# The decay of the first two heads of a linear attention is queued behind the projection of the keys instead of that of the values

## The chip, the cores and the metric

The kernel runs on one core of a Trainium2 chip. The metric is the time of one execution on the device in microseconds (us). The core has TensorE (PE; its weight loads are shown apart as PEld), VectorE (DVE), ScalarE (ACT), GpSimd (POOL) and SyncE (SP), which issues most transfers. Each engine works through its own list of instructions in order, and waits for the others through semaphores.

## The reference, cut to what matters

One decoder layer on 256 tokens of width 2048. Two kinds of attention read one projection of the normalised input: four heads of gated linear attention (GLA) and eight heads of a sparse attention (NSA). Their outputs go through one output projection, and a feed-forward block follows. Everything is float32.

```python
n = rms_norm(x, attn_norm_g)
proj = n @ w_in
(g_qkv, g_lr, g_out, nq, kc, vc, ks, vs, kw, vw, ng) = jnp.split(proj, offsets, axis=-1)
g_qkv = jax.nn.silu(causal_short_conv(g_qkv, gla_conv_w))
gq, gk, gv = jnp.split(g_qkv, [GLA_QK, 2 * GLA_QK], axis=-1)
gla_out = gla_mixer(gq, gk, gv, g_lr, g_out, gla_gate_w2, gla_gate_b, gla_norm_g)
nsa_out = nsa_mixer(nq, kc, vc, ks, vs, kw, vw, ng, ...)
h = x + jnp.concatenate([gla_out, nsa_out], axis=-1) @ w_out
m = rms_norm(h, ffn_norm_g)
return h + (jax.nn.silu(m @ w_gate) * (m @ w_up)) @ w_down
```

In the GLA, a gate gives every key channel a logarithmic decay for each token, `log_a`. A score between a query at t and a key at s is a product of their channels, weighted by the exponential of the decay summed from s to t:

```python
b = jnp.cumsum(gi, axis=2)
decay = jnp.exp(jnp.where(causal, b[:, :, :, None, :] - b[:, :, None, :, :], -jnp.inf))
scores = jnp.einsum('bhtd,bhsd,bhtsd->bhts', qi, ki, decay)
o_intra = jnp.einsum('bhts,bhse->bhte', scores, vi)
```

So the decay needs the gate, and its product with queries and keys needs those two; it needs no values. The values enter with `o_intra`.

## The kernel before

**Matrix products.** Each float32 matrix product is made of three passes: operands are split into a high part (hi) and a rest (lo), and hi x hi, hi x lo and lo x hi are added in PSUM. A projection (`proj`, L291) covers 512 columns of the weights: for 16 blocks of 128 rows and 2 blocks of 128 tokens it issues three matmuls, 96 in all, each 512 columns wide. Weights come in raw tiles of 4 row blocks (tag "raw", 3 buffers, loaded by SP at L128), and `split` (L131) makes for every 2 row blocks a hi tile on ACT (L137) and a lo tile on DVE (L138), with 4 buffers each. A raw buffer is free when its lo parts are made, and a hi or lo buffer when TensorE is done with it.

**Order of the projections.** The low-rank gate with half of the output gate; the other half of the output gate; queries; keys; first half of the values; second half of the values (these are columns 0, 512, 1024 and 1536); then for the NSA the keys of the compression, of the selection and of the window, and two halves of the queries. Then comes the output projection in two halves (`w_out_half`): the first reads the GLA's outputs, the second those of the NSA. After that comes the feed-forward block.

**Side work.** All else is written as generators that hand back control at each `yield`. `drive` (L98) runs the projections; every matmul yields 2 units, and whenever the credit reaches the pace, `side` (L83) advances one generator by one step: the first in the list `urgent`, or, when that is empty, the first in the list `later`. At pace 1.5 a projection offers 128 steps, at 2.5 76.8. Where both lists are empty, steps pass unused. A third list, `background`, is advanced by a count of units of its own: `sum_rows` loads weights of the feed-forward block on SP (L1041), adds rows of them on DVE (L1046) and stores the sums by POOL (L1050).

**Planner.** The generators only set the order in which instructions are written down. A planner of the framework then places them on their engines: an instruction that is ready may go ahead of earlier written ones that are not. Tiles of one tag share a number of buffers. The tag "g2" (a 4 KB-and-smaller working tile of SBUF) has 13.

**The GLA around the change.** `gla_gate` (L428) is in `later` from the first projection on; it leaves the gate's logarithms in `dec["f"]`, and `dec["r"]` zeroed. After queries, keys and each half of the values, `conv` (L481) is put in `urgent`: it turns the projection on TensorE, runs the short convolution (L490 on ACT, L492 on DVE) and ends with Silu on ACT, in `to_qk` (L500; L502 and L503) and, for values, `to_v` (L507; L510 and L511), which turns them back (L521). `gla_decay(hp)` (L526) serves the heads 2 hp and 2 hp + 1. For 7 block lengths it takes two Exp on ACT (L542, L544), updates running sums r and f on DVE (L548, L550) and multiplies by keys and queries on DVE (L552 or L554, L555), with two steps of nothing after each half: 28 steps, and one more for the part across chunks (L560 to L564). It fills 8 tiles of the tag "g2". It issues no matmul and no DMA. `gla_scores` (L567) multiplies these tiles on TensorE (L581) and picks blocks on DVE (L576); `gla_out` (L599) multiplies by the values (L604 to L608); `gla_turn` (L625) turns the result for the output projection. `gla_mix` (L644) runs all this for four heads: the decay of heads 0 and 1, four empty steps, then scores and outputs, with the decay of heads 2 and 3 interleaved with the scores of head 1.

**Where it is queued.** `gla_mix` enters `later` after the second half of the values, before the NSA projections begin. There, `compress` (L736) is put behind it, and `nsa_mix` (L917) after that. At the end of the first half of the output projection both lists are drained, so all of it must be written by then.

Of the kernel before, what the change touches and what calls it, by code (L numbers as in the profile page):

```python
# [33 lines left out]
C_LR, C_GO, C_NQ, C_KC, C_KS, C_KW, C_NG = 2048, 2064, 3088, 4112, 4624, 5136, 5648  # L34
# [3 lines left out]
def kernel(  # L38
# [30 lines left out]
    def bank():  # L69
        n_tiles[0] += 1  # L70
        return pp.tile([P, 512], F32, tag="bank", name=f"bank_{n_tiles[0]}")

    def behind(op):

        return tc.issue_after(op.ins) if op is not None else nullcontext()
# [5 lines left out]
    urgent, later, background = [], [], []  # L81

    def side():  # L83

        for queue in (urgent, later):
            while queue:
                try:
                    next(queue[0])
                    return
                except StopIteration:  # L90
                    queue.pop(0)
# [6 lines left out]
    def drive(mains, pace):  # L98

        credit = 0.0  # L100
        for m in mains:
            for units in m:
                count[0] += units
                if background and 0 < rate[0] <= count[0]:
                    count[0] = 0
                    if next(background[0], None) is None:
                        background.pop(0)
                credit += units
                while credit >= pace:
                    side()  # L110
                    credit -= pace
# [19 lines left out]
    def split(r, nk, w, k0=0, fine=False):  # L131

        res = []
        for k in range(k0, nk, 2):
            h, o = weight("hi", 2, w, 4), weight("lo", 2, w, 4)
            for i, n in ((0, 1), (1, 1)) if fine else ((0, 2),):
                act(h[:, i:i + n], r[:, k + i:k + i + n], AF.Copy)  # L137
                last["d"] = TT(o[:, i:i + n], r[:, k + i:k + i + n], f32(h[:, i:i + n]), ALU.subtract)  # L138
            res += [(h[:, 0], o[:, 0]), (h[:, 1], o[:, 1])]
        return res  # L140

    def fetch(mat, k0, nk, c0, w):
        return load(mat[k0 * P:(k0 + nk) * P, c0:c0 + w].rearrange("(k p) w -> p k w", p=P), nk, w)
# [65 lines left out]
    def transpose(o, i, n=P):  # L209
        return nc.tensor.transpose(o, i, ident[:n, :n])  # L210
# [80 lines left out]
    def proj(c0, evac, parts=((0, 512),), start=None):  # L291

        w = parts[-1][0] + parts[-1][1]
        banks = [[bank()[:, :pw] for _ in range(NT)] for _, pw in parts]
        ws = start(0) if start else None
        for q in range(NQ):
            if not start:
                ws = split(fetch(wi, 4 * q, 4, c0, w), 4, w)
            for i, u in enumerate(chunk(banks, n_h[q], n_l[q], ws, q == 0, q == 3, parts)):
                yield u  # L300
                if start and q == 0 and i == 5:
                    with behind(last["mm"]):
                        next(first_rest)
                if start and i == (12 if q == 0 else 6) and q < 3:
                    with behind(last["mm"] if q == 0 else None):
                        nxt = start(q + 1)
            if start and q < 3:
                ws = nxt
        evac(banks)
# [64 lines left out]
    def ev_go(b):  # L374
        def f(banks):
            if b == 0:
                lr = small([NT, 16])
                for t in range(NT):
                    TS(lr[:, t, :], banks[0][t][:, 0:16], rx[:, t:t + 1], None, ALU.mult)
            for t in range(NT):  # L380
                at = 0
                for bk in banks:
                    src = bk[t][:, 16:] if b == 0 and at == 0 else bk[t]
                    n = src.shape[1]
                    act(gout[b][:, t, at:at + n], src, AF.Silu, scale=rx[:, t:t + 1])
                    at += n
            if b == 0:
                later.append(gla_gate(lr))
        return f
# [72 lines left out]
    kk, qq = (g4([2, 2, 2, P]) for _ in range(2))  # L462
# [12 lines left out]
    def scaled(banks):  # L475
        u = g4([NT, 512])
        for t in range(NT):
            act(u[:, t, :], banks[0][t], AF.Copy, scale=rx[:, t:t + 1])
        return u
# [15 lines left out]
    def ev_conv(ct, dst):  # L495
        def f(banks):
            urgent.append(conv(scaled(banks), ct, dst))
        return f

    def to_qk(near, far):  # L500
        def f(pair, y):
            act(near[:, pair, 0 if near is kk else 1], y[:, :, 0:P], AF.Silu)  # L502
            act(far[:, pair, 0 if far is qq else 1], y[:, :, S - 1:P - 1:-1], AF.Silu)  # L503
            yield
        return f

    def to_v(b):  # L507
        def f(pair, y):
            v = g2([2, S])
            act(v[:, :, 0:P], y[:, :, 0:P], AF.Silu)  # L510
            act(v[:, :, P:], y[:, :, S - 1:P - 1:-1], AF.Silu)  # L511
            c0 = (4 * b + 2 * pair) * P
            for _ in range(10):
                yield
            p = bank()
            for t in range(NT):
                for c in range(2):
                    transpose(p[:, t * S + c * P:t * S + (c + 1) * P], v[:, c, t * P:(t + 1) * P])
                yield
            for t in range(NT):  # L520
                nc.scalar.copy(v_sb[t][:, c0:c0 + 2 * P], p[:, t * S:(t + 1) * S])  # L521
        return f
# [3 lines left out]
    def gla_decay(hp):  # L526

        e = dec[hp] = {}

        def cut(a, l):  # L530
            return a.rearrange("p b h (n r i) -> p (b h n) r i", r=2, i=l)

        def blocks(a):
            return a.rearrange("p (b n) i -> p b n i", b=2)

        f_, r_ = (dec[name].rearrange("p c s -> p (c s)").rearrange("p (g b h s) -> p g b h s", g=2, b=2, h=2)[:, hp] for name in "fr")
        k_, q_ = kk[:, hp], qq[:, hp]
        for l in LEVELS:
            e[l] = g2([2, 2, P])
            f, r, q, k, ev = (cut(a, l) for a in (f_, r_, q_, k_, e[l]))  # L540
            n = f.shape[1]
            act(ev[:, :, 1, :], f[:, :, 1, :], AF.Exp, scale=1.0 / TAU)  # L542
            if l > 1:
                act(ev[:, :, 0, :], r[:, :, 0, :], AF.Exp, scale=1.0 / TAU)  # L544
            yield
            yield
            to, ends = blocks(r[:, :, 0, :]), blocks(f[:, :, 1, l - 1:l])[:, ::-1]
            TT(to, to, ends.to_broadcast([P, 2, n // 2, l]), ALU.add)  # L548
            if 2 * l < P:
                TT(f[:, :, 1, :], f[:, :, 1, :], f[:, :, 0, l - 1:l].to_broadcast([P, n, l]), ALU.add)  # L550
            if l > 1:
                TT(ev[:, :, 0, :], ev[:, :, 0, :], k[:, :, 0, :], ALU.mult)  # L552
            else:
                nc.vector.tensor_copy(ev[:, :, 0, :], k[:, :, 0, :])  # L554
            TT(ev[:, :, 1, :], ev[:, :, 1, :], q[:, :, 1, :], ALU.mult)  # L555
            yield
            yield
        off, first_g = g2([2, 2, P]), small([2, 1])
        e["off"] = off
        TS(first_g, f_[:, 0, :, 0:1], 1.0 / TAU, None, ALU.mult)  # L560
        act(off[:, 0], r_[:, 0], AF.Exp, scale=1.0 / TAU)
        for h in range(2):
            act(off[:, 1, h], r_[:, 1, h], AF.Exp, scale=1.0 / TAU, bias=first_g[:, h])
        TT(off, off, k_, ALU.mult)  # L564
        yield
# [77 lines left out]

    def gla_mix():  # L644
        res = [{} for _ in range(4)]
        yield from gla_decay(0)
        for _ in range(4):
            yield
        nxt = iter(())
        for h in range(4):  # L650
            if h == 1:
                nxt = gla_decay(1)
            if h == 2:
                yield from nxt
            for _ in gla_scores(h, res[h]):
                yield
                next(nxt, None)
            if h:
                yield from gla_out(h - 1, res[h - 1])
        for _ in range(7):  # L660
            yield
        yield from gla_out(3, res[3])
# [579 lines left out]
    def down_last():  # L1242
# [68 lines left out]
        for t, bk in enumerate((banks[4], at[1])):  # L1311
# [5 lines left out]
    constants()  # L1317
    background += [sum_rows(f, pair) for f in sorted(SUMS) for pair in SUMS[f]]
    rate[0] = 12
    drive([proj(C_GO + 512, ev_go(1)), proj(0, ev_conv(0, to_qk(qq, kk))), proj(512, ev_conv(4, to_qk(kk, qq))),  # L1320
           proj(1024, ev_conv(8, to_v(0))), proj(1536, ev_conv(12, to_v(1)))], 1.5)
    later.append(gla_mix())
    rate[0] = 30
    drive([proj(C_KC, ev_kc), proj(C_KS, ev_kv(0)),
# [52 lines left out]
```

## Time and profile before

| | |
|---|---|
| median of 3 runs | 1111.65 us (1109.31, 1111.65, 1111.91) |
| the profiled execution's own time | 1109.58 us |
| its span, first to last instruction | 1107.9 us |
| PE busy | 1097.7 us (99%) |
| PEld busy | 900.7 us (81%) |
| DVE busy | 991.5 us (89%) |
| ACT busy | 741.5 us (67%) |
| granted TensorE clock | 1.00 |

A group's row names line, engine, operation, tiles and shapes, then the count, busy time, mean of one in ns, and the idle time of the engine just before, with what ended it. A row of waits is: engine, line and tile that waited, what it waited for, total us, times, longest us. A row of the timeline begins with its start from the span's begin and its duration. A row of a stretch gives for each engine its busy time there and, in brackets, the number of instructions, then the granted clock, the share of the DMA engines and GB/s. Matmuls overlap, so a PE that counts as busy may still be slowed; waits and the number of matmuls in a stretch show that.

### The profile page before, as it was taken

To read this page: it belongs to the slowest core of one execution; us is meant where nothing else is said; L and a number is where in the kernel's file an instruction comes from. 1 tells how busy PE (TensorE), PEld (TensorE's weight loads), DVE (VectorE), ACT (ScalarE), POOL (GpSimd) and SP (SyncE) were. 2 spreads that over 40 slices of the span, in tenths; PEclk is the share of its full clock that TensorE was granted. 3 is DMA by queue.
4 is the path that set the end of the run, shared out by engine and by line. 5 is a ranking of instruction groups with operands and counts; after the bars stand their busy time and mean duration, and the time that the engine had idled before them with its cause. 6 is when DMAs were issued, how large, how long until landed. Compare 5 with 4: busy or idle time off the path is not lost.

```text
span 1107.9 us, 14624 instructions
## 1 busy us (share of the span) xinstructions
PE 1097.7 (99%) x5298; PEld 900.7 (81%) x5298; DVE 991.5 (89%) x1277; ACT 741.5 (67%) x1009; POOL 74.0 (7%) x139
## 2 busy tenths in 40 slices
PE   9999999999999999999999999999999999999998
PEld 8888887897777887888888888888888888887886
DVE  6678779987589788997999999999999999999997
ACT  7645557555566586667586866768586866767684
POOL 4110000123101000000000000000000000000000
PEclk9999999999999999999999999999999999999999
DMA  7999985568846656785565657576566657476663
GB/s 272 336 337 361 368 285 187 188 227 286 282 183 225 218 185 215 244 305 202 192 223 198 217 197 251 187 248 212 206 228 213 213 197 255 167 267 220 234 229 114
DMA packets 124850, 259.61 MB, mean 234 GB/s; under 512 B 6709, under 2 KB 8793, under 8 KB 124778
## 3 DMA queue, kind: packets, MB, share of 16 engines
q1 hardware_dynamic: 113514, 219.86, 57.3%
q0 software_dynamic: 10368, 37.75, 9.2%
q10 hardware_dynamic: 896, 1.07, 0.3%
q8 instruction: 41, 0.67, 0.2%
q14 instruction: 31, 0.25, 0.1%
HBM read 239.78 MB, written 18.87 MB: 233 GB/s over the span
## 4 chain that ended last, share of the span: by engine, by line
PE 83%; DVE 6%; DMA 6%; issue 2%; ACT 2%; SPq 0%; POOL 0%; ACTq 0%; POOLq 0%; DVEq 0%
PE bank L283 39%; PE bank L1114 35%; DMA raw<-in_w_in_dram 3%; PE bank L210 3%; DMA g<-in_w_up_dram 2%; PE bank L1255 2%; DVE ftwo L639 2%; DVE lo L138 2%; PE bank L913 1%; PE bank L850 1%; ACT hi L137 1%; PE bank L581 1%; DMA fraw<-in_w_down_dram 1%; DVE g L1145 0%; DVE g L1046 0%
## 5 line engine op out<-in xcount | busy, mean ns | idle before, releaser
L1114 PE MATMUL bank<-ftwo,g 128*128 128x512 f32 x1848 | 431.6, 392 | 0.2 <-ACT ftwo L638 0.2
L1114 PEld LDWEIGHTS bank<-ftwo,g 128*128 128x128 f32 x1848 | 342.4, 188 | 76.6 <-DVE ftwo L639 3.5
L283 PE MATMUL bank<-hi,g 128*128 128x512 f32 (+1 forms) x1088 | 321.7, 375 | 1.3 <-ACT hi L323 1.3
L639 DVE TENSOR_TENSOR ftwo<-fraw,ftwo 128x1536 fp32r<-128x1536 f32 (+1 forms) x130 | 257.6, 1982 | 9.0 <-ACT ftwo L638 7.6
L638 ACT ACTIVATE ftwo<-fraw 128x1536 fp32r<-128x1536 f32 (+1 forms) x130 | 217.0, 1671 | 32.7 <-DMA fraw<-in_w_up_dram 13.8
L283 PE MATMUL bank<-ftwo,g 128*128 128x512 f32 x960 | 221.4, 391 | 1.0 <-ACT bank L1226 1.0
L283 PEld LDWEIGHTS bank<-hi,g 128*128 128x128 f32 x1088 | 192.4, 188 | 31.4 <-ACT hi L323 1.7
L283 PEld LDWEIGHTS bank<-ftwo,g 128*128 128x128 f32 x960 | 179.2, 188 | 40.5 <-ACT bank L1226 3.1
L283 PE MATMUL bank<-lo,g 128*128 128x512 f32 (+3 forms) x544 | 194.5, 377 | 0.0
L137 ACT ACTIVATE hi<-raw 128x1024 fp32r<-128x1024 f32 (+3 forms) x124 | 130.7, 1057 | 90.5 <-PE bank L283 74.3
L138 DVE TENSOR_TENSOR lo<-raw,hi 128x1024 fp32r<-128x1024 f32 (+3 forms) x124 | 150.1, 1217 | 38.0 <-ACT hi L137 37.3
L638 ACT ACTIVATE ftwo<-g 128x1024 fp32r<-128x1024 f32 x74 | 78.2, 1057 | 69.0 <-DVE g L1145 43.7
L283 PEld LDWEIGHTS bank<-lo,g 128*128 128x128 f32 x544 | 98.6, 189 | 15.9 <-issue 0.8
L639 DVE TENSOR_TENSOR ftwo<-g,ftwo 128x1024 fp32r<-128x1024 f32 x74 | 90.2, 1219 | 10.7 <-ACT ftwo L638 10.7
L639 DVE TENSOR_TENSOR ftwo<-fsum,ftwo 128x1024 fp32r<-128x1024 f32 x74 | 90.1, 1217 | 0.0
L638 ACT ACTIVATE ftwo<-fsum 128x1024 fp32r<-128x1024 f32 x74 | 77.5, 1048 | 8.6 <-DVE fsum L1147 7.4
L1238 ACT COPY g<-bank 128x512 f32<-128x512 f32 x80 | 45.9, 589 | 39.7 <-PE bank L283 37.8
L1145 DVE TENSOR_TENSOR g<-fraw 128x1024 f32<-128x1024 f32 x56 | 67.4, 1217 | 0.0
L1226 ACT COPY bank<-g 128x512 f32<-128x512 f32 x80 | 45.2, 592 | 13.1 <-DVE f L1175 11.5
L638 ACT ACTIVATE g<-bank 128x512 fp32r<-128x512 f32 (+1 forms) x50 | 29.2, 592 | 36.2 <-PE bank L210 29.0
L1103 POOL DMA_DIRECT2D g<-sums x16 | 8.5, 533 | 512.1 <-DVE ftwo L639 482.3
L210 PE MATMUL bank<-ident,g 128*128 128x128 f32 (+2 forms) x214 | 40.1, 278 | 1.2 <-DVE g L814 0.5
(241 smaller groups left out, 902.2 us busy)
## 6 DMA issues: line engine op xcount, KB each, us to landing
fraw<-in_w_gate_dram SPq DMA_DIRECT2D x86, 512.0 KB, 3.8
fraw<-in_w_down_dram SPq DMA_DIRECT2D x42, 1024.0 KB, 5.0
raw<-in_w_in_dram SPq DMA_DIRECT2D x36, 1024.0 KB, 7.5
fraw<-in_w_up_dram SPq DMA_DIRECT2D x70, 512.0 KB, 4.6
sums<-g POOLq DMA_DIRECT2D x32, 512.0 KB, 6.5
raw<-in_w_out_dram SPq DMA_DIRECT2D x16, 1024.0 KB, 5.3
g<-in_w_gate_dram SPq DMA_DIRECT2D x16, 512.0 KB, 8.4
g<-in_w_up_dram SPq DMA_DIRECT2D x16, 512.0 KB, 8.6
```

The source lines that it names most:

```text
L137: act(h[:, i:i + n], r[:, k + i:k + i + n], AF.Copy)
L138: last["d"] = TT(o[:, i:i + n], r[:, k + i:k + i + n], f32(h[:, i:i + n]), ALU.subtract)
L210: return nc.tensor.transpose(o, i, ident[:n, :n])
L283: last["mm"] = mm(bk[t], a[:, k, t * P:(t + 1) * P], m[:, off:off + w], start=(first_ and k == 0 and i == 0), stop=(end and k == 3 and i = ...
L581: mm(p[:, j * P:(j + 1) * P], u, w, start=True, stop=True)
L638: act(hi, ps, AF.Copy)
L639: last["d"] = TT(lo, ps, f32(hi), ALU.subtract)
L1114: mm(banks[q], x, m, start=todo[q] == total[q], stop=todo[q] == 1)
L1145: TT(s1, r[:, 1:3], r[:, 3:4].to_broadcast([P, 2, 512]), ALU.add)
L1226: nc.scalar.copy(banks[qs[n][t]], h_sb[n][:, t, :])
L1238: nc.scalar.copy(h_sb[n][:, t, :], bs[t])
L1255: mm(bk, u, m, start=(first and i == 0), stop=(end and i == 2), skip_group_check=onto)
```

## The change

The decay of heads 0 and 1 leaves `gla_mix`, together with the four empty steps behind it. It enters `later` as a generator of its own, right after the projection of the keys. For this the call of `drive` over five projections is cut into two, at the same pace; the credit left at the cut is zero in both versions. Nothing of what is computed changes.

```diff
     def gla_mix():
         res = [{} for _ in range(4)]
-        yield from gla_decay(0)
-        for _ in range(4):
-            yield
         nxt = iter(())
         for h in range(4):
             if h == 1:
...
     rate[0] = 12
-    drive([proj(C_GO + 512, ev_go(1)), proj(0, ev_conv(0, to_qk(qq, kk))), proj(512, ev_conv(4, to_qk(kk, qq))),
-           proj(1024, ev_conv(8, to_v(0))), proj(1536, ev_conv(12, to_v(1)))], 1.5)
+    drive([proj(C_GO + 512, ev_go(1)), proj(0, ev_conv(0, to_qk(qq, kk))), proj(512, ev_conv(4, to_qk(kk, qq)))], 1.5)
+    later.append(gla_decay(0))
+    drive([proj(1024, ev_conv(8, to_v(0))), proj(1536, ev_conv(12, to_v(1)))], 1.5)
     later.append(gla_mix())
```

## The prediction

> **What bounds the kernel now.** I read the page first, then busy time by stretch, then the waits of TensorE.
>
> ```profile
> span 1107.9 us, 14624 instructions
> PE 1097.7 (99%) x5298; PEld 900.7 (81%) x5298; DVE 991.5 (89%) x1277; ACT 741.5 (67%) x1009; POOL 74.0 (7%) x139
> ...
> PE 83%; DVE 6%; DMA 6%; issue 2%; ACT 2%; SPq 0%; POOL 0%; ACTq 0%; POOLq 0%; DVEq 0%
> ```
>
> TensorE sets the time: 83% of the chain is PE. The change adds and removes no instruction on it, so it can pay or cost only what TensorE waits. By the count of projection matmuls in the trace (96 each), the projections run on TensorE as follows: first values 104 to 126.5 us, second values to 150.5, compression keys to 175.8, selection keys to 208.
>
> ```profile
> core 0: us, PE busy (x) PEld busy (x) DVE busy (x) ACT busy (x) POOL busy (x), PEclk, DMA share, GB/s
> 104.00:126.50 22.50, 22.50 (x105) 18.61 (x104) 19.28 (x29) 12.36 (x19) 2.24 (x5) 1.00 1.04 390
> 126.50:150.50 24.00, 24.00 (x114) 19.44 (x113) 19.11 (x27) 14.18 (x23) 1.60 (x3) 1.00 0.89 306
> 150.50:170.00 19.50, 19.50 (x93) 15.89 (x91) 14.19 (x21) 11.24 (x18) 0.53 (x1) 1.00 0.84 280
> 170.00:190.00 20.00, 18.71 (x105) 15.04 (x104) 19.63 (x56) 16.05 (x35) 0.53 (x1) 1.00 0.61 206
> 190.00:215.00 25.00, 24.71 (x143) 21.08 (x141) 23.27 (x56) 15.38 (x35) 2.47 (x2) 1.00 0.40 133
> 215.00:240.00 25.00, 25.00 (x193) 24.38 (x192) 20.33 (x48) 11.52 (x26) 4.21 (x5) 1.00 0.74 253
> ```
>
> VectorE (DVE) is full from 170 to 190 us (19.63 of 20), and only there does PE's busy time fall visibly short of the stretch. The waits say for what; the first row is of the weight loads (PEld) in the stretch 100:165, the next five of those in 165:215, the seventh of those in 215:290; the last is of PE itself in 165:215.
>
> ```profile
> PEld bank L210 <- ACT g L510: 0.9, 3, 0.3
> ...
> PEld bank L581 <- DVE g L555: 2.5, 3, 1.7
> PEld bank L283 <- DVE lo L138: 0.8, 2, 0.4
> PEld bank L210 <- DVE g L714: 0.5, 1, 0.5
> PEld bank L210 <- ACT g L510: 0.2, 1, 0.2
> PEld bank L581 <- DVE g L564: 0.2, 1, 0.2
> ...
> PEld bank L210 <- DVE g L814: 0.9, 1, 0.9
> ...
> PE bank L581 <- DVE g L555: 1.3, 1, 1.3
> ```
>
> The score matmuls of head 0 (L581) wait for the last step of the decay (L555). That is the stall which the moved step causes today. The projections of the values (100 to 165 us) hold hardly any wait.
>
> **What moves.** A projection yields 96 times, two units each. At pace 1.5 that is 192/1.5 = 128 side steps. During the first values' projection the queue holds the convolution of the keys (14 steps) and then nothing. The change puts the 29 steps of the first decay there: 14 + 29 = 43 of 128. At pace 2.5 (76.8 steps per projection) the rest of the linear attention, then the compression, then the sparse attention come 29 + 4 = 33 steps earlier, 33 x 1.25 = 41 matmuls. In the first half of the output projection (192 steps, of which 189 are used now) 36 steps at the end become empty. The decay has no DMA and no matmul. It is moved past both value convolutions and the splits of weights around them, on ACT and DVE. SP is touched indirectly: its loads of raw weights wait for the split (L138) that frees their buffer.
>
> Emission is not yet the order on the engines: the planner pulls ready work ahead. This row is a decay step, over 100 us before the rest of its decay:
>
> ```profile
> 57.16 0.42 DVE L548 TENSOR_TENSOR g<-g,g 128x256 f32<-128x256 f32 x1
> ```
>
> Between ready instructions the earlier emitted one goes first. While decay and scores ran, the splits that TensorE needs came late: rows of L138 alone, same stretches as above.
>
> ```profile
> 104.00:126.50 22.50, 9.66 (x9) 1.00 1.04 390
> ...
> 170.00:190.00 20.00, 3.36 (x3) 1.00 0.61 206
> ```
>
> **Cost of the moved work.** Rows of DVE and ACT in 170:184.4, then two of the DVE timeline.
>
> ```profile
> L555 DVE TENSOR_TENSOR g<-g,g 128x256 f32<-128x256 f32 x7 | 2.9, 419 | 0.1
> L550 DVE TENSOR_TENSOR g<-g 128x256 f32<-128x256 f32 x6 | 2.5, 420 | 0.2 <-ACT g L542 0.2
> L548 DVE TENSOR_TENSOR g<-g,g 128x256 f32<-128x256 f32 x6 | 2.5, 419 | 0.0
> L552 DVE TENSOR_TENSOR g<-g,g 128x256 f32<-128x256 f32 x6 | 2.5, 417 | 0.0
> L564 DVE TENSOR_TENSOR g<-g,g 128x512 f32<-128x512 f32 x1 | 0.7, 693 | 0.1
> ...
> L542 ACT ACTIVATE g<-g 128x256 f32<-128x256 f32 x8 | 3.4, 428 | 0.5 <-DVE g L550 0.4
> L544 ACT ACTIVATE g<-g 128x256 f32<-128x256 f32 x6 | 2.5, 419 | 0.5 <-DVE g L548 0.5
> L542 ACT ACT_TABLE_LOAD x1 | 1.3, 1283 | 0.0
> ```
> ```profile
> 178.10 0.42 DVE L550 TENSOR_TENSOR g<-g 128x256 f32<-128x256 f32 x1 [0.21 <-ACT g L542]
> ...
> 181.80 0.42 DVE L552 TENSOR_TENSOR g<-g,g 128x256 f32<-128x256 f32 x1
> ```
>
> Back to back these start every (181.80 - 178.10)/11 = 0.336 us. So the decay takes 25 x 0.336 + 0.7 + one small copy (0.2 by estimate) = 9.3 us of DVE and about 5.9 us of ACT.
>
> *What is removed.* The wait for L555 in PE itself, 1.3 us, goes: the decay would be done some 45 us ahead of the scores. The other waits of 165:215 come from the same full DVE, now short of 9.3 us of work: 2.5 - 1.7 = 0.8, and 0.8 + 0.5 + 0.2 + 0.2, together 2.5 us. These are idle times of weight loads, which partly lie under running matmuls (1.7 there was 1.3 in PE), and the second decay moves up into the same place. I take 1.1 of the 2.5. Gain: 2.4 us; bounds 1.3 (the one wait) and 1.3 + 2.5 + 0.9 (the L814 wait, if the earlier compression clears that too) = 4.7 us.
>
> *What is added.* The first values' stretch has 22.5 - 19.28 = 3.2 us of DVE idle, and the decay needs 9.3. So 6.1 us of other DVE work slips. What slips is what was emitted later: splits of weights, and the background sums (L1046). The rows are, in order, of the chain of waits, of the groups on ACT and DVE in 104:126.4, and of the ACT and DVE timelines.
>
> ```profile
> 84.42 21.13 PE bank L283 x93
> ...
> L137 ACT ACTIVATE hi<-raw 128x1024 fp32r<-128x1024 f32 x8 | 8.4, 1057 | 8.7 <-DMA raw<-in_w_in_dram 5.1 <-PE bank L283 2.3 <-issue 1.3
> ...
> L1046 DVE TENSOR_TENSOR g<-g 128x512 f32<-128x512 f32 x4 | 2.8, 688 | 0.9 <-DMA g<-in_w_up_dram 0.9
> L1046 DVE TENSOR_TENSOR g<-g,g 128x512 f32<-128x512 f32 x4 | 2.7, 685 | 0.0
> ...
> 113.13 1.06 ACT L137 ACTIVATE hi<-raw 128x1024 fp32r<-128x1024 f32 x1 [1.29 <-issue]
> ...
> 117.00 2.35 DVE L138 TENSOR_TENSOR lo<-raw,hi 128x1024 fp32r<-128x1024 f32 x2
> ```
>
> A matmul takes 21.13/93 = 0.227 us, a pair of weight rows serves 12, so 2.72 us. Four pairs of buffers let a split begin three pairs (8.2 us) before its use. The pair whose high part starts at 113.13 is due at 121.3; its low part starts at 117.00 and takes 1.2, so the lead is down to about 3 us, the least of this projection. Cover: that lead, and 5.5 us of background sums, for which nothing in this stage waits. If all sums gave way, 3.2 + 5.5 = 8.7 of 9.3 us would be covered and PE would lose nothing. If the splits gave way as they did at 170 us (three in 20 us), the decay runs from the key's Silu at 114.8 for about 12 us with one split inside. The next ends near 128 where 123.8 is due: 4.7 us with rounding. I take 1.1, nearer the lower end, because the planner has idle and sums to spend first. Sums that slip hold their buffers longer; SP's next background load may then wait ahead of raw weights. ACT already waits 5.1 us for weights here, so that is part of the upper bound.
>
> *Table switches.* Exp now lies between the Silu of the keys and of the values: at least two loads more, 2 x 1.28 = 2.6 us of ACT. ACT has 22.5 - 12.36 = 10.1 us idle there, less 5.9 for the Exp = 4.2 us, so nothing, while the planner doesn't alternate Exp and Silu.
>
> The Trainium skill ("ScalarE: Activation LUTs", What ACT_TABLE_LOAD costs) gives 2.66 us for a switch, 1.28 of load and 1.38 of drain, and its rule is to batch by table set; that speaks against this change. By it two switches are 5.3 us, 1.1 more than the idle, which the lead still covers.
>
> In the row above a load takes 1.28, and the sum stays by it.
>
> *Sum.* The profiled execution took 1109.58 us (span 1107.9 and 1.7 around it): 1109.58 - 2.4 + 1.1 = 1108.3, or 1.3 less. It stands 2.1 below the median of 1111.65. So I forecast 1110.4 us, no difference that a measurement of this kernel can tell: the three runs lie 2.6 us apart, and about 0.3% (3.3 us) is what it tells.
>
> **Rivals.**
>
> A, all waits come back and none is added: -4.7, 1107.0 us. For it: the values' projections have hardly a wait. [...]
>
> B, slower: in the first values' projection the decay goes ahead of L138 on DVE, and TensorE waits for the low parts. It decides once a split is late by more than 3 us. Price 4.7, with only the 1.3 of L555 returned: +3.4, 1115.1 us. For it: the three splits in 170:190. Against: the decay alternates ACT and DVE, so splits find gaps.
>
> C, ACT becomes the bound there: Exp is ready while Silu of the second key pair is not, and the planner alternates. Six loads are 7.7 us against 4.2 idle; 3.5 late, of which the lead of 3 is then used up, so the 1.1 of DVE delay grows by 3.5: -2.4 + 4.6 = +2.2, 1113.9 us.
>
> By the price of a switch in the Trainium skill ("ScalarE: Activation LUTs", What ACT_TABLE_LOAD costs; 2.66 us) six would be 16.0 us, an estimate, and the stall near 12; no row here shows the drain in it.
>
> D, the planner puts the decay where it was, because its tiles still queue behind others: 1111.65 us. The step pulled to 57 us shows that emission doesn't fix place.
>
> **Chances.** Forecast 0.50, with its own range 1108 to 1113; A 0.24, B 0.15, C 0.06, D 0.05. Faster than 1108.3: A and a small part of the forecast, 0.28. Slower than 1115.0: B mostly, 0.16. Same: 0.56. The range takes in A and B with a margin of the runs' spread: 1106.0 to 1115.5.
>
> **What would show it.** Right: L542 and L555 of the first decay between 107 and 130 us; no wait of L581 for L555 near 177; DVE in 104:126.5 above 22 us and clearly below 19.63 in 170:190; two or more table loads extra. B shows as PEld waits for L138 between 115 and 130, C as ACT with four loads or more there. Wrong: a PE wait over 3 us at any place named under no step, above all in the sparse attention, which I hold at no change though it starts 33 steps earlier.

## The result and the profile after

The changed kernel took 1117.74 us in the median of four runs (1117.03 to 1117.95), the kernel before 1111.14 us beside it (1109.31 to 1111.91): a ratio of 1.0061, 95% interval 1.0043 to 1.0078. It is slower by 6.6 us, where 1.3 us of gain was forecast, and it lies above the predicted range. The profiled execution took 1117.03 us.

The page of the changed kernel (span, busy time, share of the chain of waits by engine):

```profile
span 1115.3 us, 14630 instructions
...
PE 1101.3 (99%) x5298; PEld 902.3 (81%) x5298; DVE 992.7 (89%) x1277; ACT 745.8 (67%) x1013; POOL 73.6 (7%) x139
...
PE 78%; DVE 8%; DMA 7%; ACT 3%; issue 3%; SPq 1%; POOL 0%; ACTq 0%; DVEq 0%; POOLq 0%
```

The work is the same: matmuls and VectorE instructions are equal in number, and ACT has four more, which are table loads. TensorE's share of the chain fell from 83% to 78%; what it lost went to DVE (6% to 8%), DMA, ACT, issue and SP, about one point each. Busy time by stretch, in the prediction's windows (PE, PEld, DVE, ACT, POOL, clock, DMA):

```profile
104.00:126.50 22.50, 18.54 (x85) 14.72 (x83) 22.04 (x49) 19.81 (x36) 1.33 (x3) 1.00 0.87 324
126.50:150.50 24.00, 23.89 (x103) 19.38 (x104) 19.15 (x26) 12.69 (x18) 1.59 (x3) 0.93 0.87 297
...
170.00:190.00 20.00, 19.75 (x114) 16.46 (x112) 17.10 (x49) 14.04 (x31) 1.35 (x2) 1.00 0.50 160
```

The decay did move: DVE is now full in 104:126.5 (22.04 for 19.28 before) and lighter in 170:190 (17.10 for 19.63). The stretch that had no idle TensorE now has four microseconds of it: PE fell from 22.50 to 18.54. The waits of TensorE itself (not of its weight loads) in the stretches 100:165, 165:300 and 300:380, one row for what was waited for (us, times, longest):

```profile
PE bank L283 <- DVE lo L138: 4.1, 1, 4.1
PE bank L210 <- ACT g L510: 1.3, 1, 1.3
...
PE bank L210 <- DVE g L711: 0.7, 1, 0.7
PE bank L210 <- DVE g L622: 0.2, 1, 0.2
...
PE bank L210 <- ACT g L856: 0.9, 1, 0.9
PE bank L210 <- DVE sm L860: 0.3, 1, 0.3
PE bank L283 <- DVE g L639: 0.2, 1, 0.2
```

The same view of the kernel before, 165:300, beside the row of L555 that the prediction shows; 100:165 and 300:380 have no row there:

```profile
PE bank L210 <- DVE g L814: 0.5, 1, 0.5
PE bank L210 <- DVE g L714: 0.3, 1, 0.3
```

(Lines from the edit on are three lower in the changed kernel: L814 is L811 there, L714 is L711, L1046 is L1043.)

The wait of L581 for L555 is gone. In its place stands a wait of 4.1 us for a split of weights (L138) in the projection of the first values. Three timelines show how it came about. DVE of the changed kernel:

```profile
115.89 1.22 DVE L138 TENSOR_TENSOR lo<-raw,hi 128x1024 fp32r<-128x1024 f32 x1
117.02 0.69 DVE L1043 TENSOR_TENSOR g<-g 128x512 f32<-128x512 f32 x1
117.62 0.42 DVE L548 TENSOR_TENSOR g<-g,g 128x256 f32<-128x256 f32 x1
...
119.63 0.69 DVE L1043 TENSOR_TENSOR g<-g,g 128x512 f32<-128x512 f32 x1
...
121.58 0.69 DVE L1043 TENSOR_TENSOR g<-g,g 128x512 f32<-128x512 f32 x1
...
125.00 0.42 DVE L555 TENSOR_TENSOR g<-g,g 128x256 f32<-128x256 f32 x1
125.33 1.22 DVE L138 TENSOR_TENSOR lo<-raw,hi 128x1024 fp32r<-128x1024 f32 x1
```

Between the two splits lie 8.3 us with nothing but 19 steps of the decay and three background sums. ACT had made the high part of the late pair long before:

```profile
117.40 1.05 ACT L137 ACTIVATE hi<-raw 128x1024 fp32r<-128x1024 f32 x1
```

So its low part could have begun at 118.45, and it began at 125.33. (This is the pair whose high part the prediction quotes at 113.13. Here ACT makes it 4.3 us later, behind two table loads, the Silu of the keys and two Exp; what that lateness costs is taken up at e2 and e8.) TensorE, in the same trace:

```profile
120.97 1.57 PE L283 MATMUL bank<-hi,g 128*128 128x512 f32 x5
126.61 0.80 PE L283 MATMUL bank<-lo,g 128*128 128x512 f32 x1 [4.07 <-DVE lo L138]
127.20 0.63 PE L283 MATMUL bank<-hi,g 128*128 128x512 f32 x1
```

The matmuls behind the first one after the wait start about 0.42 us apart (127.20, 127.63, 128.05), where 0.227 is usual. By stretch (the column behind the busy times is the granted clock):

```profile
122.00:126.60 4.60, 0.54 (x2) 0.11 (x1) 4.55 (x12) 3.35 (x9) 0.00 (x0) 1.00 0.24 98
126.60:130.10 3.50, 3.49 (x8) 2.81 (x9) 3.50 (x5) 0.00 (x0) 0.53 (x1) 0.52 0.16 23
130.10:132.00 1.90, 1.90 (x10) 1.56 (x9) 1.87 (x3) 1.07 (x1) 0.00 (x0) 1.00 0.96 273
```

For 3.5 us after the wait the granted clock was 0.52. Eight matmuls took 3.49 us, not 8 x 0.227 = 1.82: another 1.7 us, which shows as busy time and in no view of waits. The Trainium skill ("TensorE: Matmul & The Clock Gate", Part 1) says that an idle TensorE falls to half clock and needs some 3.4 us of work to come back; this stretch agrees.

The account: the waits of PE come to 7.7 us after (seven rows) and 2.1 us before (0.5 + 0.3, and 1.3 for L555); the difference of 5.6 and the 1.7 of slow clock are 7.3 of the 7.4 us by which the span grew. These rows leave out what lies before 100 and behind 380 us. Counted by number, the same projection matmul comes 0.15 us later than before at 104 us, 7.7 us later at 371 us, and stays within 0.4 us of that up to the end, so the loss does lie between. By place: +5.8 in the first values' projection (4.1 + 1.7), +1.3 for L510 in the second, -1.3 for L555, +0.1 in the projections after it, +1.4 in the sparse attention at 319 to 321 us.

### The profile page after: what moved, and what is told of

Same layout as the page of the kernel before. It is cut to its first block, busy times and chain, and to the rows that moved or that the text cites. A ratio compares the mean times of both kernels' runs of the same rounds, so it can differ in the third digit from the quotient of the medians.

```text
span 1115.3 us, 14630 instructions
## 1 busy us (share of the span) xinstructions
PE 1101.3 (99%) x5298; PEld 902.3 (81%) x5298; DVE 992.7 (89%) x1277; ACT 745.8 (67%) x1013; POOL 73.6 (7%) x139
## 4 chain that ended last, share of the span: by engine, by line
PE 78%; DVE 8%; DMA 7%; ACT 3%; issue 3%; SPq 1%; POOL 0%; ACTq 0%; DVEq 0%; POOLq 0%
PE bank L283 36%; PE bank L1111 35%; DMA g<-in_w_up_dram 3%; DMA raw<-in_w_in_dram 3%; PE bank L210 2%; DVE lo L138 2%; PE bank L1252 2%; DVE ftwo L639 2%; PE bank L910 1%; ACT hi L137 1%; DVE g L1043 1%; DMA fraw<-in_w_down_dram 1%; DVE g L639 0%; DMA raw<-in_w_out_dram 0%; DVE g L492 0%
## 5 line engine op out<-in xcount | busy, mean ns | idle before, releaser
L639 DVE TENSOR_TENSOR ftwo<-fraw,ftwo 128x1536 fp32r<-128x1536 f32 (+1 forms) x130 | 258.0, 1985 | 8.5 <-ACT ftwo L638 7.3
L137 ACT ACTIVATE hi<-raw 128x1024 fp32r<-128x1024 f32 (+3 forms) x124 | 130.6, 1056 | 101.9 <-PE bank L283 80.7
L138 DVE TENSOR_TENSOR lo<-raw,hi 128x1024 fp32r<-128x1024 f32 (+3 forms) x124 | 150.5, 1219 | 41.6 <-ACT hi L137 40.7
L639 DVE TENSOR_TENSOR ftwo<-g,ftwo 128x1024 fp32r<-128x1024 f32 x74 | 90.3, 1221 | 10.6 <-ACT ftwo L638 10.6
L639 DVE TENSOR_TENSOR ftwo<-fsum,ftwo 128x1024 fp32r<-128x1024 f32 x74 | 90.3, 1220 | 0.0
```

Of the source, the lines that this page charges most:

```text
L639: last["d"] = TT(lo, ps, f32(hi), ALU.subtract)
```

## The experiments

All start from the changed kernel. The theory to be tested: the late split is a matter of order on DVE (decay steps and sums ahead of a split that is due), and a smaller part of the loss comes from the rest of the attention, which now runs 33 steps earlier. Against it stood: the DVE simply has too much to do there; ACT's table loads are to blame; the early rest is free. Ratios are to the kernel before, on the same chip.

| run | what differs from the changed kernel | median us | ratio, 95% |
|---|---|---|---|
| e1 | rest in its old place | 1115.20 | 1.0040 (1.0026 to 1.0053) |
| e2 | sums paused in the first values, made up at once | 1118.06 | 1.0064 (1.0049 to 1.0079) |
| e3 | Exp behind the keys' last Silu | 1113.00 | 1.0021 (1.0012 to 1.0031) |
| e4 | decay spread, six empty steps behind each | 1111.52 | 1.0011 (1.0002 to 1.0021) |
| e5 | e4, and rest in its old place | 1109.36 | 0.9996 (0.9987 to 1.0005) |
| e6 | e5, and Exp behind the Silu | 1109.33 | 0.9997 (0.9989 to 1.0006) |
| e7 | decay 82 steps later | 1113.60 | 1.0037 (1.0022 to 1.0052) |
| e8 | sums paused, made up slowly | 1115.80 | 1.0053 (1.0038 to 1.0069) |
| e9 | e4, and the sparse attention alone in its old place | 1108.82 | 0.9982 (0.9973 to 0.9990) |
| e10 | e7, and rest in its old place | 1111.87 | 1.0012 (1.0003 to 1.0021) |
| e11 | decay spread by three steps, rest in its old place | 1112.77 | 1.0018 (1.0008 to 1.0028) |

### e1: the rest where it was

```diff
     def gla_mix():
         res = [{} for _ in range(4)]
+        for _ in range(33):
+            yield
```

> The decay of heads 0 and 1 sits behind the keys as in the changed kernel, but 33 empty steps stand at the head of gla_mix, so that all that is queued behind it is written where it was before. Theory 1 (the cost is local: in the first values' projection the split of the seventh pair of weight rows stands on DVE behind a burst of decay steps, TensorE waits 4.1 us for it and then runs at about half its clock for 3.5 us): the wait stays between 3 and 5 us and the time is 5 to 8 us above before. Theory 2 (the cost comes from the rest moving 33 steps earlier): no more than 1 us above before.

The stall is there unchanged. TensorE's timeline of e1:

```profile
126.34 0.79 PE L283 MATMUL bank<-lo,g 128*128 128x512 f32 x1 [4.07 <-DVE lo L138]
```

So the larger part of the loss belongs to the moved decay alone, and the ratios of the changed kernel and e1 lie 0.21% (2.3 us) apart: a first sign, no more since the intervals overlap, that the early rest isn't free. The time of e1, 0.40% (4.4 us) over the kernel before, lies just under theory 1's 5 to 8 us and far above theory 2's 1 us.

### e2 and e8: without the background sums

e2 stops the sums in the first values' projection and makes them up in the second; e8 makes them up slowly, over the keys of the sparse attention.

```diff
-    drive([proj(1024, ev_conv(8, to_v(0))), proj(1536, ev_conv(12, to_v(1)))], 1.5)
+    rate[0] = 0
+    drive([proj(1024, ev_conv(8, to_v(0)))], 1.5)
+    rate[0], count[0] = 6, 0          # e8: 12
+    drive([proj(1536, ev_conv(12, to_v(1)))], 1.5)
+    count[0] = 0                      # e8: rate[0] = 18 instead of 30 for the keys
```

> The changed kernel, with the background sums paused during the first values' projection and run at twice the rate during the second. DVE is spared 3 sums (1.8 us) inside the burst, and the planned order then has the split of the seventh pair after 4 decay steps instead of about 22. Theory 1 (DVE order): no wait of TensorE for L138 above 1.5 us in the first values' projection, the TensorE clock stays full, and the time is within 3 us of before. Theory 3 (ScalarE is what is late: two table loads between the Exp of the decay and the Silu of the keys): the loads are still there, the high parts stay about 4 us late, and a wait of 2 to 4 us stays.

> The background sums are paused in the first values' projection and made up slowly afterwards (18 for 30 of the pace, over the projections of keys), so DVE has 5.5 us less to do in the place of the stall; the decay stays where the change has it. Theory 1 (order: decay steps and sums stand ahead of the split that is due): the burst ahead of that split is 12 decay steps and no sum, 4.0 us against a lead of about 3 to 4: wait at 126.6 under 1 us, and the slow matmuls behind it go; without the crowd of made-up sums the wait of 4.7 us at 170 that came with the quick making up goes too: 1112 to 1114. Rival (the sums of the later stages always pay, wherever they go): a wait of 2 us or more in the projections of keys, 1116 to 1118.

In both the wait at 126.6 is gone: neither has a wait of PE between 100 and 165 us. The table loads there are the same three as in the changed kernel, so they did not cause it alone. Nor did the late high part alone: it is as late in e2 and e8. The rows of e8, its high part on ACT and its low part on DVE:

```profile
117.60 1.05 ACT L137 ACTIVATE hi<-raw 128x1024 fp32r<-128x1024 f32 x1
118.77 1.22 DVE L138 TENSOR_TENSOR lo<-raw,hi 128x1024 fp32r<-128x1024 f32 x1
```

The whole decay is still in this projection (its last instruction on DVE, L564, is at 127.22 us, in the changed kernel at 126.47). But only 4 decay steps now stand ahead of that split, then 4 and 10 ahead of the next two, where there were 19 and three sums. So a decay that lies in this projection need not stall TensorE.

No time was won, though, and e2's expectation (within 3 us of the kernel before) was missed: 7.1 us by the ratio. In e2 TensorE stops in the projection of the compression keys instead:

```profile
170.29 1.97 PE L210 MATMUL bank<-ident,g 128*128 128x128 f32 x8 [4.58 <-ACT g L510]
```

In e8 the stops come later still, mostly in the queries' projections (its waits of PE in 165:300):

```profile
PE bank L210 <- DVE g L711: 2.3, 2, 1.5
PE bank L210 <- DVE g L768: 1.4, 1, 1.4
```

e8 missed its expectation (1112 to 1114) and came near the rival's: the sums cost time in both of the places to which they were put off. The prediction counted them as cover. They are work without a reader in this stage, but not without a cost. Neither run isolates 2 us of DVE, since the planner orders everything anew when the sums are absent.

### e3 and e6: the table loads

```diff
+            with behind(last["silu"]):
                 act(ev[:, :, 1, :], f[:, :, 1, :], AF.Exp, scale=1.0 / TAU)
```

(and the same for the other Exp; `last["silu"]` is the keys' last Silu.)

> The changed kernel, with the Exp of the decay ordered behind the last Silu of the keys on ScalarE, so that Exp and Silu don't alternate inside the first values' projection: two table loads fewer (2.6 us of ScalarE). In the planned order on DVE the splits also stand between shorter bursts, with one burst of about 11 decay steps left (3.7 us). Theory 1: the wait shrinks to 0 to 2 us, time 0 to 3 us above before. Theory 3: the wait goes as well. The run tells the two apart only together with e4_spread6.

> As the run beside it (decay spread over the values' projections, rest in its old place), and the Exp of the decay is held behind the last Silu of the keys, so that ACT changes its table set less often. Theory: table loads cost nothing here since ACT has idle time (4.2 us in the first values' projection by the prediction's rows): time within 1 us of the run beside it, with two to four loads fewer. Rival C' (the loads, 1.28 us each, delay the high parts and the values' evacuation): 1 to 3 us faster than the run beside it, and the waits for L510 and L137 shorter.

The table loads of e5's sibling without this edit, e4, in 100:180 (busy us, mean ns, idle before), and then those of e6:

```profile
L542 ACT ACT_TABLE_LOAD x4 | 5.1, 1283 | 0.1
...
L510 ACT ACT_TABLE_LOAD x2 | 2.6, 1283 | 1.1 <-DVE g L492 1.1
L502 ACT ACT_TABLE_LOAD x1 | 1.3, 1283 | 0.0
```
```profile
L543 ACT ACT_TABLE_LOAD x3 | 3.8, 1283 | 0.0
L510 ACT ACT_TABLE_LOAD x2 | 2.6, 1283 | 0.4 <-DVE g L492 0.3
```

Seven loads in e4, five in e6. e5, which has e4's seven, and e6 have the same time (1109.36 and 1109.33). Table loads cost nothing that can be told here, as the prediction held. That e3 takes 1113.0 us and not 1117.7 is thus better put down to its other effect: the decay starts later, and in place of the wait of 4.1 us come two, 1.1 and 0.4 us, for L138 in the second values' projection, with no wait for L510 behind them.

### e4 and e11: how much stands ahead of the split

```diff
+    def spread(g, n):
+        for _ in g:
+            yield
+            for _ in range(n):
+                yield
-    later.append(gla_decay(0))
+    later.append(spread(gla_decay(0), 6))     # e11: 3, and the 33 empty steps of e1
```

> The changed kernel, with 6 empty steps behind each of the 29 steps of the decay, so that it is written across both values' projections; the planned order has at most 8 decay steps between two splits on DVE, and Exp and Silu alternate more often (two table loads more than in the changed kernel). Theory 1: no wait of TensorE for L138 above 1 us, time within 2 us of before, or up to 2 us below it since the wait of the scores for the decay (1.3 us) is gone. Theory 3: the wait stays at 4 us or grows, time 6 us or more above before.

> Three empty steps behind each decay step instead of six, rest in place. In the planned order some 11 decay steps and three sums then stand ahead of the split that was late in the change, where 22 and three did. Theory 1 (what stands ahead of that split on VectorE sets the wait, step by step): 11 steps fewer are 11 x 0.336 = 3.7 us, so the wait of 4.2 us shrinks to some 0.5 and the slow matmuls behind it go: 1109.4 to 1110.5, same as before. Rival (the stall hangs on the decay lying in this projection at all): 4 us of wait, 1115.

With six empty steps (e4) no wait of PE is left between 100 and 165 us, although DVE is as full in the first values' projection as in the changed kernel, 22.08 us for 22.04 (columns as above):

```profile
104.00:126.50 22.50, 22.50 (x104) 18.39 (x103) 22.08 (x41) 18.84 (x31) 1.72 (x4) 1.00 1.00 351
```

So a full DVE alone does not stall TensorE there. What differs is what is put ahead: ahead of the split that was late stand three sums, as before, but only 4 decay steps. e11 is the dose between. Its DVE timeline around the split, and then its TensorE:

```profile
115.19 1.22 DVE L138 TENSOR_TENSOR lo<-raw,hi 128x1024 fp32r<-128x1024 f32 x1
...
122.05 0.42 DVE L555 TENSOR_TENSOR g<-g,g 128x256 f32<-128x256 f32 x1
122.38 2.35 DVE L138 TENSOR_TENSOR lo<-raw,hi 128x1024 fp32r<-128x1024 f32 x2
```
```profile
123.65 0.50 PE L283 MATMUL bank<-lo,g 128*128 128x512 f32 x1 [1.50 <-DVE lo L138]
...
154.02 0.44 PE L210 MATMUL bank<-ident,g 128*128 128x128 f32 x2 [2.37 <-ACT g L510]
```

Between the two splits stand twelve decay steps and three sums here, against 19 and three in the changed kernel and in e1. (The expectations of e7 and e11 count 22 and 11; the timelines give 19 and 12.) Seven steps fewer are 7 x 0.336 = 2.4 us, and the wait shrank from e1's 4.07 to 1.50, by 2.6. The decay begins on DVE as early as in e1 (L550 at 108.88 us for 109.18) and ends 2.5 us later (L564 at 128.74 for 126.20), the rest is in the same place, and the wait follows what is ordered ahead of the split. The expected time (1109.4 to 1110.5) was missed all the same, since a wait of 2.4 us for L510 came in the second values' projection, which none of the theories had.

Nor did e4, free of both, beat the kernel before, although L555's 1.3 us is gone there. Its waits of PE in 165:300 and 300:380:

```profile
PE bank L210 <- ACT g L510: 1.1, 1, 1.1
PE bank L210 <- DVE g L717: 0.7, 1, 0.7
PE bank L610 <- DVE g L582: 0.4, 1, 0.4
...
PE bank L210 <- ACT g L862: 0.9, 1, 0.9
PE bank L210 <- DVE sm L866: 0.3, 1, 0.3
PE bank L283 <- DVE g L645: 0.2, 1, 0.2
```

The gain turned into new waits. The last three are those of the changed kernel at 319 to 321 us (L856, L860, L639 there).

### e5 and e9: which part of the rest pays

e5 adds the 33 empty steps of e1 to e4. e9 adds them at the head of the sparse attention only:

```diff
     def nsa_mix():
...
+        for _ in range(33):
+            yield
         for i, u in enumerate(tiles):
```

> The decay is spread as in the run before (six empty steps behind each of its steps, no wait in the values' projections there) and 33 empty steps stand at the head of the rest, so that the sums of values, the compression and the sparse attention keep their old places. Theory M (the rest pays for coming 33 steps earlier: 1117.7 for the change against 1115.2 with the rest held in place, and 1111.5 for the spread decay with the rest early): the waits of 1.2 us at 175 (L510 behind the eviction of the compression keys on ACT) and 0.8 us at 218 (L712) go, and with them about 2 us: 1109 to 1110, at or just under the kernel before (1110.4 to 1111.6), because L555's wait of 1.3 us stays away too. Rival N (the 2.5 us between those two runs belonged to the stalled values' projection alone): 1111.5 as with the rest early, same as before.

> The decay is spread with six empty steps; the scores of the linear attention and the compression come early as in the change, but 33 empty steps stand at the head of the sparse attention, which so comes at its old place in the output projection. Theory S (the early sparse attention pays: three waits near 320 us of 1.1, 0.4 and 0.3 us in the change and in the spread run with the rest early, none with the rest in place): these go, 1111.5 - 1.8 = 1109.7. Rival L (the early scores and compression pay: waits of 0.6 us for L582 and 0.8 us for L717 in place of two of 0.3, and 1.2 for 0.6 at 175): 1111 to 1111.5, as with everything early.

e5 is level with the kernel before, 0.15% (1.7 us) under e4 by the ratios, whose intervals overlap by 0.03%. e9 is clearer: with scores and compression early and only the sparse attention in its old place, the time is 1108.82 us, 0.29% (3.2 us) under e4 with no overlap, and 0.18% (0.10% to 0.27%) under the kernel before: the one version that beats both kernels. Its waits of PE in 165:300 are word for word the first three rows of e4 above, and for 300:380 there is no row. So the first three waits of e4 stayed, the last three vanished. They are 1.4 us of the 3.2; these rows don't show the rest. So it is the early sparse attention that pays; the early scores and compression cost nothing that these runs can tell (e5, with all of the rest in its old place, is no faster than e9). Why the sparse attention finds ACT and DVE late when it comes 33 steps earlier was not tried.

### e7 and e10: the decay later

```diff
+    def wait(n, g):
+        for _ in range(n):
+            yield
+        yield from g
-    later.append(gla_decay(0))
+    later.append(wait(82, gla_decay(0)))      # e10: and the 33 empty steps of e1
```

> The decay queues 82 steps later than in the change: its first step is issued when the splits of the first values' projection are nearly all issued, and the rest of the attention follows it as in the change. Theory 1 (the split of weights due at 121.3 us was late because 22 decay steps and three sums stood ahead of it on DVE): the wait at 126.6 and the eight slow matmuls behind it go, 4.1 + 1.6 us; decay steps then stand ahead of a split in the second values' projection, with the lead of that place (3 to 8 us) against bursts of some 12 steps (4.0 us): a wait of 0 to 2 us there, and with the rest early about 2 us more as before: 1111 to 1114. Rival (the wait belongs to DVE's total work in the two projections, not to the place of the decay): a wait of 4 us appears in the second values' projection, 1117 again.

> The decay queues 82 steps later than in the change, as in the run of 1113.6, and the rest of the attention stays in its old place. The rest early costs 2 to 2.5 us by the two pairs run so far, so 1111.1 to 1111.6 by theory M. What is then left over the kernel before is the wait of 2.2 us for L510 at 152.8 and its slow matmuls, less the 1.5 us of L555. Rival N (early rest costs only beside the other two kernels): 1113.6 again.

The wait for the split is 0.4 us (e7) and 0.3 us (e10), and both fell within the expected times or 0.3 us beside them. Both have a wait of 2.0 us for L510 at the end of the second values' projection, as e11 has 2.4 and the changed kernel 1.3. In the changed kernel and in e11 ACT stands idle there for the convolution on DVE (2.38 and 1.85 us before L510). DVE, in the changed kernel:

```profile
152.41 0.69 DVE L1043 TENSOR_TENSOR g<-g 128x512 f32<-128x512 f32 x1 [1.34 <-DMA g<-in_w_up_dram]
153.01 0.48 DVE L492 SCALAR_TENSOR_TENSOR g<-bank,cols,g 128x254 f32<-128x254 f32 x1
```

The sum stands ahead of the values' convolution on DVE and waits for its own transfer. The planner had put it there; a load of background work that comes late holds up work that is due. In e7 and e10 it isn't the sum: the last convolution ends ahead of it, at 151.85 us in e7, behind a split on DVE, and ACT, which works without a gap on an eviction (L478) and a high part (L137) from 150.14 on, comes to L510 at 152.35. e10 and e7 differ by 0.25% (2.8 us), the third pair that says the early rest costs; a part of it is the clock, below: of e7's four runs the two with a mean granted clock of 1.000 took 1112.69 and 1112.75 us, the two with 0.998 and 0.996 took 1114.45 and 1115.73.

## Why the prediction was wrong

**What bounds, and what moves: right.** TensorE set the time, and the change acted only through its waits. The signs named for the move are there: L542 from 109.10 and L555 from 114.87 us, no wait of L581 for L555, DVE at 22.04 and 17.10, four table loads more.

**The gain: half right.** The 1.3 us of L555 came back, as its lower bound said. The further 1.1 taken from neighbouring waits did not: L714's 0.3 became 0.7, and L814's 0.5 went, but 0.2 for L622 and 1.3 for L510 came. The same DVE was less full there, yet a lighter stretch only moves the place where something is last.

**The added wait: the step that failed.** I took 1.1 us, bounds 0 to 4.7, "because the planner has idle and sums to spend first". It did spend the idle (DVE 22.04 of 22.50), but not ahead of the splits: three sums, 2.1 us, went ahead of the late split along with the decay, and the number of splits made in the stretch fell from nine to five. The wait was 4.1 us. What decided was not whether DVE had room in the projection (e4 fills DVE as much there, 22.08 us, and has no wait; in e8 the decay lies in the same projection and has none) but how much stands in one run ahead of a split whose lead is 3 us: 19 steps and three sums in the change, 12 and three in e11, 4 and three in e4, 4 and none in e8. The rows for this were on hand: the prediction quotes the three splits in 170:190, where the same decay held them back, and gave that reading the smaller chance.

**A cost with no term.** The 1.7 us of half clock behind the wait stood in no sum. It takes the added cost to 5.8 us, above its upper bound.

**The early rest: the second miss.** I held the sparse attention "at no change": there came 1.4 us of new waits in the sparse attention (e4 against e9), by the pairs of runs 1.7 to 3.2 us in all. The prediction named this as the place to look.

**Rivals.** B, at 0.15, had mechanism and place right: L138 late in the first values, only L555 returned. Its wait was 4.7 for a measured 4.1; its time, 1115.1, lacks the clock (1.7) and the new waits for L510 and in the sparse attention (1.3 + 1.4), and with these it would have come to 1119.5, or 1118.9 with the measured wait, for 1117.7. That its price lies so near is in part luck: its own figures, 128 less 123.8, give 4.2 and not 4.7, and they are for the next pair of rows; the split that came late was that of the pair it took to be covered by the lead of 3 us. C had the alternating Exp and Silu right (four loads more) and their effect wrong (e2, e5, e6). A and D are out.

**Open.** What sets the planner's choice among ready instructions, which keeps a split behind 19 decay steps. A fifth pair of hi and lo buffers, which would lengthen the lead, wasn't tried.

## What to carry to other kernels

Free time of an engine over a stage says little about whether added work fits; ask how long a run of it can stand ahead of the one instruction that TensorE needs next, and hold that against its lead. Work that fits over a stage is best added in small pieces (here six empty steps behind each), and what follows it should keep its place until a run shows that it may come earlier. Add to a wait of several microseconds on TensorE what the clock takes behind it.

## What the hardware showed

The price of a wait depends on more than its length. e10 and e7 have the same wait of 2.03 us for L510 at the same place of the same code. For each, the row of TensorE's timeline and then the stretch of 3.5 us behind it; e7 first:

```profile
152.81 0.44 PE L210 MATMUL bank<-ident,g 128*128 128x128 f32 x2 [2.03 <-ACT g L510]
```
```profile
152.80:156.30 3.50, 3.49 (x12) 2.86 (x13) 3.33 (x5) 0.91 (x3) 0.53 (x1) 0.60 1.05 367
```

Then e10:

```profile
153.07 0.44 PE L210 MATMUL bank<-ident,g 128*128 128x128 f32 x2 [2.03 <-ACT g L510]
```
```profile
153.00:156.50 3.50, 3.43 (x19) 2.83 (x19) 3.39 (x5) 0.96 (x4) 0.53 (x1) 1.00 1.10 364
```

In e7 12 matmuls ran in that time, at a clock of 0.60; in e10 19, at full clock. After e11's 2.37 us the clock was full too; in the 3.5 us after the waits of 4.07 (changed kernel, e1) and 4.58 us (e2) it was 0.52, 0.57 and 0.50. Shorter waits close to each other can do it as well. The three waits at the early sparse attention, 0.9, 0.3 and 0.2 us, left the clock at 1.00 in the changed kernel; in the profiled run of e3, which has them too, this stretch lies behind them:

```profile
316.00:318.00 2.00, 2.00 (x6) 1.51 (x6) 2.00 (x3) 2.00 (x8) 0.00 (x0) 0.50 1.03 390
```

One kernel goes both ways: five of e3's ten runs had a mean granted clock of 0.998 and took 1113.26 to 1114.66 us, the other five had 0.999 or 1.000 and took 1111.67 to 1112.74. The medians lie 1.7 us apart, as much as the slow matmuls behind the wait cost the changed kernel.

The Trainium skill ("TensorE: Matmul & The Clock Gate", Part 1) says that the window in which idleness is judged runs freely, so that its phase differs from run to run; e3's runs and the pair of e7 and e10 agree with that. The same part gives a window of about 3.4 us of idleness for the fall to half clock; here the measurements differ, since 2.03 us were enough in e7, and 1.4 us in three waits in e3.

The spread of times goes with this: of the 29 runs of the kernel before that e9 was compared with, five had a mean granted clock of 0.998, and took 1111.77 to 1112.67 us; the others took 1108.22 to 1112.01, in the median about 1110.2. All 11 of e9 had 0.999 or 1.000, and took 1108.22 to 1109.70. So a part of e9's gain, 2.0 us by the ratio, goes with the clock: against the median of the others it is about 1.3 us, and by the two profiled executions alone, spans of 1106.8 and 1107.9 us, 1.1 us. Behind which wait the clock falls in those five isn't shown.
